# First FFN of a hybrid decoder step: weight sums on VectorE instead of GpSimd, and down pieces handed out three behind four products

## Chip, cores and metric

The kernel runs on one core of one Trainium2 chip. The metric is the device time of one execution in microseconds (us). A core has TensorE (PE in the rows, with PEld for its weight loads), VectorE (DVE), ScalarE (ACT), GpSimd (POOL) and SyncE (SP, whose queue issues the weight loads). Each engine works through its own instructions in the order in which they stand.

## The reference, cut to what matters

One layer of a decoder is computed for 512 prompt tokens and 32 sample tokens (544 columns together) with a model width of 1024. The change lies in the first of the two feed-forward blocks:

```python
def swiglu(x, wg, wu, wd):
    return (jax.nn.silu(x @ wg) * (x @ wu)) @ wd
...
    h = h + 0.5 * rmsnorm(swiglu(rmsnorm(h, norm_g[0]), wg[0], wu[0], wd[0]), norm_g[1])
```

`wg` and `wu` are 1024 x 2816 and `wd` is 2816 x 1024, all float32. The mixer (a gated linear recurrence and a latent attention over a paged cache), its output projection and a second feed-forward block follow; the change does not touch their code.

## The kernel before

**Precision.** A float32 matrix product is made of three fast products. Each operand is split into a high part (ScalarE copies it to the type `F32R`) and a low part (VectorE subtracts the high part from the source), and high x high, high x low and low x high are added up in PSUM. The helper `split` does it, at lines 168 (ScalarE) and 169 (VectorE).

**The first FFN by block products.** Tokens lie on the free axis in two halves of 272 columns. Hidden columns are taken in pairs of tiles, 256 of them, `j` = 0 to 10. For each `j` there are two calls of `tile_pair`, one for the gate weights `w_g` (result in `G`, tile `ha` or `hb`) and one for the up weights `w_u` (result in `V`). For `j` = 0 and 1 the product is made directly (`classic`). From `j` = 2 (`WARM`) on, `seven` makes the 2 x 2 block product of (2 weight tiles x 2 halves of the contraction) with (2 halves of the contraction x 2 token halves) from seven products instead of eight. That needs sums and differences of weight blocks: `S[:,0]`, `S[:,1]`, the difference left in `w2[:, lo4]`, and the one left in `w1[:, hi4]`. These are four instructions of 128 x 512, at lines 567, 568, 569 and 573. The rows call them `S<-wraw`, `S<-S,wraw`, `wraw<-wraw` and `wraw<-wraw,S`.

There are 18 calls of `seven`. Each splits its weights (`a`: `w1` itself; `s`: the two sums; `v`: `w2`; `s4`: the last difference), runs seven products into the PSUM banks `X`, `Y` and `Z`, and moves them out: `tq<-X` on ScalarE, and five additions on VectorE by `plus` (line 585: `ha<-Y,tq`, `ha<-Z,ha` and the like). A product is 12 matmuls of 128 x 128 by 272 columns. The order in one `seven` is X, Y, X, Y, Z, Y, Z; a bank that is written a second time waits for the `plus` that reads its first value.

**Between the products.** `gated` applies the SwiGLU gate to finished `G` and `V`: three ScalarE activations at lines 318 to 320 (`sit`), VectorE multiplications at lines 615 and 616, and a split into `hh` and `hl`. `down` multiplies finished hidden tiles by `w_d`. It is a generator: each step is one piece, 12 matmuls into the tile `dn` and one addition to `ma` or `mb` (line 561; for the first group a ScalarE copy, line 559). A group has 16 pieces; there are 4 groups, started in the middle of the `w_u` call at `j` = 2, 4, 6 and 8. `fill` stands behind each of the first six products of a `seven` and takes the next step of the waiting group. So between two starts of a group there are four calls of `seven`, 28 products, 24 fills and 16 pieces. This stretch is called a period below.

**Order.** The program is written out without loops. A scheduler sets the order of the instructions on each engine from priorities and buffers; `tc.issue_after` pins a few of them. Weights come by SyncE loads of 512 KB into the tile `wraw`, which has five buffers; a load waits until a buffer is free. `S` has two buffers. After `j` = 10 a last group of down products (line 685) ends the FFN, and the mixer's projection (`w_in`) starts.

Of the kernel before, what the change touches and what calls it, by code (L numbers as in the profile page):

```python
# [14 lines left out]
ALU = mybir.AluOpType  # L15
# [11 lines left out]
HM = max(HS)  # L27
W2 = T // 2
WARM = 2
DFF = 2816  # L30
NF = DFF // P
FCH = (((0, 6), (6, 6), (12, 6), (18, 4)), ((0, 6), (6, 6), (12, 5), (17, 5)))
# [75 lines left out]
def hybrid_step_kernel(  # L108
# [5 lines left out]
    nc = tc.nc  # L114
# [12 lines left out]
    def mk(shape, dt, tag, bufs=1, pool=None):  # L127
        return (pool or cur[-1]).tile(shape, dt, name=tag, tag=tag, bufs=bufs)
# [10 lines left out]
    def ps(name, tag="ps", own=False):  # L139
        if tag == "ps" and not own:  # L140
            tag = CYC[turns[0] % 4]
            turns[0] += 1
        return pp.tile([P, 512], F32, name=name, tag=tag, bufs=NPS[tag])
# [23 lines left out]
    def split(hi, lo, src, eng=None):  # L167
        nc.scalar.copy(hi, src)
        (eng or nc.vector).tensor_tensor(lo, src, f32(hi), op=ALU.subtract)  # L169
# [82 lines left out]
    def mm3(out, pairs):  # L252
        n = 0
        last = 3 * len(pairs) - 1
        for (ah, al), (bh, bl) in pairs:
            for a, b in ((ah, bh), (ah, bl), (al, bh)):
                nc.tensor.matmul(out, a, b, start=n == 0, stop=n == last)  # L257
                n += 1
# [32 lines left out]
    def wcols(w, k0, kt, c0, n=P):  # L291
        return w[k0 * P : (k0 + kt) * P, c0 : c0 + n].rearrange("(k p) f -> p k f", p=P)
# [130 lines left out]
    def parts(pair, ks):  # L423
        return [t[:, ks] for t in pair]
# [75 lines left out]
    lo4, hi4 = slice(0, 4), slice(4, 8)  # L500
# [10 lines left out]
    with scope("ffn0") as pool:  # L511
# [5 lines left out]
        def ring():  # L517
            spin[0] += 1
            names, p_ = ((("wh", "wl"), sb), (("sh", "sl"), sp))[spin[0] % 4 > 1]
            return [mk([P, 8, P], F32R, n, 2, pool=p_) for n in names]  # L520

        def classic(w, C):
            ws = [ring() for _ in range(2)]
            for i in range(2):
                split(*ws[i], w[i])
            for x in BOTH:
                bs = ((B11, B21), (U4, B22))[x]
                for i in range(2):
                    acc = ps("acc", "acc")[:, :W2]
                    mm3(acc, [((ws[i][0][:, k], ws[i][1][:, k]), [t[:, k % 4] for t in bs[k // 4]]) for k in range(KD)])  # L530
                    mark[0] = nc.scalar.copy(C[:, 2 * i + x], acc).ins

        def product(bank, a, b, first):
            for k in range(4):
                for n, (p, q) in enumerate(((0, 0), (0, 1), (1, 0))):
                    nc.tensor.matmul(bank, a[p][:, k], b[q][:, k], start=first and k + n == 0, stop=k == 3 and n == 2, skip_group_check=True)  # L536

        downs = []

        def fill(n=1):  # L540
            for _ in range(n):
                while downs and next(downs[0], None) is None:
                    downs.pop(0)

        def down(first, q0, hs):
            nf = 2 * len(hs)
            for _ in range(3):
                yield True
            for d in range(0, KD, 2):
                raw = mk([P, 8, P], F32, "wraw", 5, pool=sb).rearrange("p (k i) c -> p k i c", i=2)  # L550
                nc.sync.dma_start(raw[:, :nf].rearrange("p k i c -> p k (i c)"), wcols(w_d[0], 2 * q0, nf, d * P, 2 * P))
                for i in range(2):
                    w = [mk([P, 4, P], F32R, "d" + n, 2) for n in "hl"]
                    split(w[0][:, :nf], w[1][:, :nf], raw[:, :nf, i])
                    for x in BOTH:
                        acc = ps("dn")[:, :W2]
                        mm3(acc, [((w[0][:, k], w[1][:, k]), [t[:, k % 2, x] for t in hs[k // 2]]) for k in range(nf)])
                        if first:
                            nc.scalar.copy(mT[x][:, d + i], acc)
                        else:  # L560
                            nc.vector.tensor_tensor(mT[x][:, d + i], mT[x][:, d + i], acc, op=ALU.add)
                        yield True

        def seven(w, C, mid=None):
            w1, w2 = w
            S = mk([P, 2, 4, P], F32, "S", 2)
            nc.gpsimd.tensor_tensor(S[:, 0], w2[:, lo4], w2[:, hi4], op=ALU.add)
            nc.gpsimd.tensor_tensor(S[:, 1], S[:, 0], w1[:, lo4], op=ALU.subtract)
            nc.gpsimd.tensor_tensor(w2[:, lo4], w1[:, lo4], w2[:, lo4], op=ALU.subtract)
            a, s, v = ring(), ring(), ring()  # L570
            for ks in (lo4, hi4):
                split(*parts(a, ks), w1[:, ks])
            nc.gpsimd.tensor_tensor(w1[:, hi4], w1[:, hi4], S[:, 1], op=ALU.subtract)
            for i, ks in enumerate((lo4, hi4)):
                split(*parts(s, ks), S[:, i])
            s4 = [mk([P, 4, P], F32R, "s4" + n, 2, pool=sp) for n in "hl"]
            with tc.issue_after(mark[0]):
                for ks in (lo4, hi4):
                    split(*parts(v, ks), w2[:, ks])
                split(*s4, w1[:, hi4])  # L580
            X, Y, Z = ps("X", "acc")[:, :W2], ps("Y", "acc")[:, :W2], ps("Z")[:, :W2]
            t = mk([P, W2], F32, "tq", 2)

            def plus(i, bank, to):
                nc.vector.tensor_tensor(C[:, i], bank, to, op=ALU.add)  # L585

            product(X, parts(a, lo4), B11, True)
            mark[0] = nc.scalar.copy(t, X).ins
            fill()
            product(Y, parts(s, hi4), T2, True)  # L590
            plus(1, Y, t)
            fill()
            product(X, parts(a, hi4), B21, False)
            nc.scalar.copy(C[:, 0], X)
            if mid:
                with tc.issue_after(mark[0]):
                    mid()
            fill()
            product(Y, parts(v, lo4), T3, False)
            plus(3, Y, t)  # L600
            fill()
            product(Z, parts(s, lo4), T1, True)
            plus(3, Z, C[:, 3])
            fill()
            product(Y, parts(v, hi4), T4, False)
            plus(2, Y, t)
            fill()
            product(Z, s4, B22, False)
            plus(1, Z, C[:, 1])
# [12 lines left out]
        def tile_pair(j, src, C, mid=None):  # L622
            if j < WARM:
                classic(pairs.pop(0) if pairs else raw_pair(src, 2 * j), C)
                if mid:
                    mid()
            else:
                seven(raw_pair(src, 2 * j), C, mid)

        for j in range(NF // 2):  # L630
            if j:
                late = G, V
            G, V = (c[:, j % 2] for c in Cq)
            if j == WARM:
                with tc.issue_after(mark[0]):
                    split(*T4, r[0])
            tile_pair(j, w_g[0], G)
            if j == WARM:
                mT = {x: actslot("m", x, n=W2) for x in BOTH}
            if j:  # L640
                H = [mk([P, 2, 2, W2], F32R, n, 3) for n in ("hh", "hl")]
                with tc.issue_after(mark[0]):
                    gated(H, *late, 0)
                hs.append(H)

            def rest():
                if j:
                    gated(H, *late, 1)
                if j in (2, 4, 6, 8):
                    fill(99)  # L650
                    downs.append(down(j == 2, j - 2, hs))

            tile_pair(j, w_u[0], V, rest)
            if j in (2, 4, 6, 8):
                hs = []
            if j == 0:
                for o, p, q in ((l[0], l[1], l[0]), (l[1], r[1], l[1]), (r[1], r[1], l[0]), (r[0], r[0], r[1])):
                    nc.vector.tensor_tensor(o, p, q, op=ALU.subtract)
                for dst, o in ((T2, r[1]), (T3, l[1]), (T1, l[0])):
                    split(*dst, o)  # L660
# [98 lines left out]
    with scope("mix") as mx_:  # L759
# [286 lines left out]
        with scope("at2"):  # L1046
# [7 lines left out]
            with scope("kv"):  # L1054
# [60 lines left out]
                for i in range(5):  # L1115
                    n = P if i < 4 else TS
# [511 lines left out]
def _arrays(inputs):  # L1628
# [10 lines left out]
        "vecs": np.ascontiguousarray(vecs),  # L1639
        "w_g": g["w_ffn_gate"].reshape(2, D, DFF),  # L1640
        "w_u": g["w_ffn_up"].reshape(2, D, DFF),
        "w_d": g["w_ffn_down"].reshape(2, DFF, D),
        "w_in": g["w_in"].reshape(D, -1),
# [22 lines left out]
```

## Time and profile before

| | |
|---|---|
| Median of 3 runs | 1302.17 us (1299.69 to 1302.77) |
| The profiled execution | 1307.5 us, of which the span is 1305.7 us |
| Busy share: PE, DVE, ACT, POOL | 97%, 75%, 57%, 14% |
| Mean granted TensorE clock | 0.993 (1.00 in every stretch of the first FFN after 20 us) |
| First product of the first `seven` | 67.53 us |
| First matmul of the last down group | 367.44 us |

Times in the trace count from the start of the span. The stretch from 67.5 to 367.4 us holds the 18 calls of `seven` and the four down groups, thus all that the change edits, but for two `seven`s' weight sums that GpSimd makes at 39 to 58 us, during `classic`. The profiled execution is 5.3 us above the median of the runs.

### The profile page before, as it was taken

What the parts mean: (1) busy time and instruction counts of PE and PEld (TensorE: products, weight loads), DVE (VectorE), ACT (ScalarE), POOL (GpSimd) and SP (SyncE); (2) the same over time, 40 slices, a digit from 0 to 9 for tenths busy, and PEclk for the clock granted to TensorE, in tenths of its full rate; (3) what the DMA queues carried; (4) which work ended last, traced back from release to release, by engine and by line L of the source; (5) the groups of instructions that cost most, each with busy time, mean ns of one, the idle gap of its engine ahead of it and who ended that gap; (6) DMA issues with size and microseconds to landing.
All of it is one profiled execution on the core that took longest, in us unless ns stands there. A gap on an engine that the chain in (4) does not pass through costs nothing.

```text
span 1305.7 us, 30361 instructions
## 1 busy us (share of the span) xinstructions
PE 1270.1 (97%) x12486; PEld 1170.7 (90%) x12486; DVE 983.5 (75%) x1897; ACT 746.1 (57%) x1578; POOL 185.0 (14%) x152
## 2 busy tenths in 40 slices
PE   7999999999999999999999999999999999999998
PEld 6989999999999988888888877777777999999997
DVE  7787777777668877776766897898987878466664
ACT  6555545454376745445658655654656777554454
POOL 0343333242100000000000422222210000000000
PEclk9999999999999999999999899999999999999998
DMA  9332323322265222323232978888776746646451
GB/s 268 109 97 81 107 89 98 94 87 79 77 188 165 76 77 74 98 76 105 83 98 82 328 231 286 273 284 260 256 250 187 224 116 181 182 143 184 142 155 53
DMA packets 280106, 197.32 MB, mean 151 GB/s; under 512 B 12830, under 2 KB 271487, under 8 KB 275615
## 3 DMA queue, kind: packets, MB, share of 16 engines
q1 hardware_dynamic: 271472, 152.11, 40.0%
q0 software_dynamic: 7168, 41.95, 8.8%
q8 instruction: 98, 1.61, 0.5%
q10 hardware_dynamic: 1326, 1.32, 0.3%
q14 instruction: 42, 0.34, 0.1%
HBM read 183.45 MB, written 11.90 MB: 150 GB/s over the span
## 4 chain that ended last, share of the span: by engine, by line
PE 82%; DVE 8%; ACT 4%; issue 3%; DMA 2%; SPq 0%; POOL 0%; DVEq 0%; ACTq 0%
PE acc L257 29%; PE acc L275 18%; PE dn L257 7%; PE Y L536 5%; PE s L1367 3%; PE X L536 3%; PE Z L536 3%; PE o L1400 3%; PE acc L685 2%; PE s L1180 1%; DVE wl L169 1%; PE pa L917 1%; PE acc L286 1%; DVE wl L249 1%; ACT wh L248 1%
## 5 line engine op out<-in xcount | busy, mean ns | idle before, releaser
L248 ACT CAST wh<-wraw 128x1024 fp32r<-128x1024 f32 (+2 forms) x194 | 185.2, 957 | 190.1 <-PE acc L257 113.2
L249 DVE TENSOR_TENSOR wl<-wraw,wh 128x1024 fp32r<-128x1024 f32 (+2 forms) x194 | 214.5, 1107 | 88.1 <-ACT wh L248 85.0
L275 PE MATMUL acc<-uha,wh 128*128 128x256 f32 (+1 forms) x528 | 159.1, 302 | 0.9 <-ACT uha L205 0.9
L275 PE MATMUL acc<-uha,wl 128*128 128x256 f32 (+1 forms) x528 | 150.4, 285 | 1.8 <-DVE wl L249 1.8
L275 PE MATMUL acc<-ula,wh 128*128 128x256 f32 (+1 forms) x528 | 151.3, 287 | 0.0
L257 PE MATMUL acc<-uhb,wh 128*128 128x288 f32 (+1 forms) x432 | 128.3, 297 | 0.1
L257 PE MATMUL acc<-ulb,wh 128*128 128x288 f32 (+1 forms) x432 | 127.7, 296 | 0.1
L257 PE MATMUL acc<-uhb,wl 128*128 128x288 f32 (+1 forms) x432 | 126.9, 295 | 0.5 <-DVE wl L249 0.3
L275 PEld LDWEIGHTS acc<-uha,wh 128*128 128x128 f32 x528 | 100.0, 190 | 15.2 <-issue 13.2
L275 PEld LDWEIGHTS acc<-uha,wl 128*128 128x128 f32 x528 | 100.0, 189 | 2.8 <-DVE wl L249 2.6
L275 PEld LDWEIGHTS acc<-ula,wh 128*128 128x128 f32 x528 | 100.4, 190 | 1.0 <-issue 1.0
L257 PEld LDWEIGHTS acc<-uhb,wl 128*128 128x128 f32 x432 | 81.2, 188 | 1.2 <-DVE wl L249 1.2
L257 PEld LDWEIGHTS acc<-uhb,wh 128*128 128x128 f32 x432 | 81.0, 187 | 0.7 <-ACT wh L248 0.3
L257 PEld LDWEIGHTS acc<-ulb,wh 128*128 128x128 f32 x432 | 81.1, 188 | 0.4 <-DVE ulb L169 0.3
L257 PE MATMUL dn<-hh,dh 128*128 128x272 f32 x256 | 73.9, 289 | 2.8 <-DVE ha L585 2.8
L257 PE MATMUL dn<-hl,dh 128*128 128x272 f32 x256 | 73.7, 288 | 0.0
L257 PE MATMUL dn<-hh,dl 128*128 128x272 f32 x256 | 73.6, 288 | 0.0
L1367 PE MATMUL s<-kh,q 64*32 64x128 f32 x2560 | 55.3, 275 | 0.6 <-issue 0.6
L1345 POOL DMA_INDIRECT rraw<-pool_r,idx x32 | 35.7, 1116 | 131.7 <-DVE kh L1355 127.3
L1391 ACT COPY pbuf<-pt 32x64 f32<-32x64 f32 x192 | 46.5, 242 | 12.8 <-DVE pt L1387 10.2
L275 PE MATMUL acc<-uhb,wh 128*128 128x272 f32 x176 | 53.2, 302 | 0.0
L257 PE MATMUL acc<-hlb,wh 128*128 128x288 f32 x176 | 52.1, 297 | 0.0
(638 smaller groups left out, 4058.6 us busy)
## 6 DMA issues: line engine op xcount, KB each, us to landing
wraw<-w_g SPq DMA_DIRECT2D x66, 512.0 KB
wraw<-w_u SPq DMA_DIRECT2D x66, 512.0 KB
wraw<-w_d SPq DMA_DIRECT2D x40, 384.0 KB
wraw<-w_in SPq DMA_DIRECT2D x24, 512.0 KB
wraw<-w_d SPq DMA_DIRECT2D x32, 320.0 KB
wraw<-w_d SPq DMA_DIRECT2D x16, 512.0 KB
wraw<-w_o SPq DMA_DIRECT2D x16, 512.0 KB
xt<-x_p SPq DMA_DIRECT2D x4, 512.0 KB
```

The source lines that it names most:

```text
L169: (eng or nc.vector).tensor_tensor(lo, src, f32(hi), op=ALU.subtract)
L248: nc.scalar.copy(wh[:, :kt], w[:, :kt])
L249: nc.vector.tensor_tensor(wl[:, :kt], w[:, :kt], f32(wh[:, :kt]), op=ALU.subtract)
L257: nc.tensor.matmul(out, a, b, start=n == 0, stop=n == last)
L275: nc.tensor.matmul(acc[:, :n], a[:, k], b[:, k], start=k + i == 0, stop=k == kt - 1 and i == 2)
L286: nc.tensor.matmul(acc, a[:, k], b[:, k], start=k + i == 0, stop=k == kt - 1 and i == 2)
L536: nc.tensor.matmul(bank, a[p][:, k], b[q][:, k], start=first and k + n == 0, stop=k == 3 and n == 2, skip_group_check=True)
L685: nc.tensor.matmul(accs[x, d], wts[d][p][:, k], hs[k // 2][q][:, k % 2, x], start=k + n == 0, stop=k == nf - 1 and n == 2)
L1345: nc.gpsimd.indirect_dma_start(rraw.rearrange("p a r -> p (a r)"), None, pool_r, off)
L1367: nc.tensor.matmul(self.s[r][c * 32 : c * 32 + 32, :P], q[rs, j], kh, start=st + jj == 0, stop=st == len(JS) - 1 and jj == 1, skip_group_c ...
L1391: (nc.scalar.copy if g else nc.vector.tensor_copy)(self.p[g * 32 : g * 32 + 32, c // 2, c % 2 * 4 : c % 2 * 4 + 4, self.i * 16 : self.i * ...
L1400: nc.tensor.matmul(o[g : g + 32, :R], self.p[:, c, a], self.craw[c][:, a], start=i + c == 0 and a < 4, stop=i + c == 2 and a >= 4, skip_gr ...
```

## The change

Two edits. First, the four weight instructions of each `seven` go from `nc.gpsimd` to `nc.vector`; their shapes, operands and place in the program text stay. Second, `fill` now gathers 0.75 of a step at each call and takes a step when a whole one is owed, so it hands out three steps behind four products. The generator `down` has one empty step ahead of its first piece instead of three, and the account `owed` is set to zero when a new group starts. A group then has 17 steps. A period's 24 fills give 18; before they gave 24 for 19 steps.

```diff
+PACE = 0.75
...
-        def fill(n=1):
-            for _ in range(n):
+        owed = [0]
+
+        def fill(n=PACE):
+            owed[0] += n
+            while downs and owed[0] >= 1:
+                owed[0] -= 1
                 while downs and next(downs[0], None) is None:
                     downs.pop(0)
...
-            for _ in range(3):
-                yield True
+            yield True
...
-            nc.gpsimd.tensor_tensor(S[:, 0], w2[:, lo4], w2[:, hi4], op=ALU.add)
-            nc.gpsimd.tensor_tensor(S[:, 1], S[:, 0], w1[:, lo4], op=ALU.subtract)
-            nc.gpsimd.tensor_tensor(w2[:, lo4], w1[:, lo4], w2[:, lo4], op=ALU.subtract)
+            nc.vector.tensor_tensor(S[:, 0], w2[:, lo4], w2[:, hi4], op=ALU.add)
+            nc.vector.tensor_tensor(S[:, 1], S[:, 0], w1[:, lo4], op=ALU.subtract)
+            nc.vector.tensor_tensor(w2[:, lo4], w1[:, lo4], w2[:, lo4], op=ALU.subtract)
...
-            nc.gpsimd.tensor_tensor(w1[:, hi4], w1[:, hi4], S[:, 1], op=ALU.subtract)
+            nc.vector.tensor_tensor(w1[:, hi4], w1[:, hi4], S[:, 1], op=ALU.subtract)
...
                     fill(99)
+                    owed[0] = 0
                     downs.append(down(j == 2, j - 2, hs))
```

The scheduler makes a new order from this on PE, DVE, ACT and SP up to the last down group; behind that, apart from a few swapped neighbours, the order is the same. Lines move down by one to five (169 is 170, 561 is 565, 567 to 569 are 571 to 573, 573 is 577, 585 is 589, 615 and 616 are 619 and 620). Three places follow.

VectorE at the start of the third down group (`j` = 6, `w_u` call). Before, from the last split of the next call's weights to the addition of the first Z:

```order
L169 TENSOR_TENSOR s4l_2719<-wraw_2695,s4h_2718 128x512
L585 TENSOR_TENSOR hb_308<-Y_2573,tq_2575 128x272
L615 TENSOR_TENSOR ha_307<-ha_307,sit_2615 128x544
L616 TENSOR_TENSOR ha_307<-ha_307,hb_308 128x544
L169 TENSOR_TENSOR wl_2706<-S_2699,wh_2705 128x512
L585 TENSOR_TENSOR hb_308<-Y_2573,tq_2575 128x272
L169 TENSOR_TENSOR hl_2532<-ha_307,hh_2531 128x544
L169 TENSOR_TENSOR wl_2706<-S_2699,wh_2705 128x512
L585 TENSOR_TENSOR hb_308<-Z_2574,hb_308 128x272
```

The same place on VectorE in the changed kernel:

```order
L170 TENSOR_TENSOR s4l_2733<-wraw_2709,s4h_2732 128x512
L589 TENSOR_TENSOR hb_308<-Y_2559,tq_2561 128x272
L619 TENSOR_TENSOR ha_307<-ha_307,sit_2615 128x544
L170 TENSOR_TENSOR dl_2771<-wraw_2649,dh_2770 128x512
L620 TENSOR_TENSOR ha_307<-ha_307,hb_308 128x544
L170 TENSOR_TENSOR wl_2720<-S_2713,wh_2719 128x512
L589 TENSOR_TENSOR hb_308<-Y_2559,tq_2561 128x272
L170 TENSOR_TENSOR hl_2518<-ha_307,hh_2517 128x544
L170 TENSOR_TENSOR wl_2720<-S_2713,wh_2719 128x512
L589 TENSOR_TENSOR hb_308<-Z_2560,hb_308 128x272
```

Between the two additions of Y stands one row more, a split for a down piece; no weight sum stands there.

VectorE one call later (`j` = 7, `w_g`), before, from the last split of the next call's weights to the second addition of Y:

```order
L169 TENSOR_TENSOR s4l_2953<-wraw_2929,s4h_2952 128x512
L561 TENSOR_TENSOR mb_922<-mb_922,dn_2743 128x272
L169 TENSOR_TENSOR dl_2831<-wraw_2828,dh_2830 128x512
L585 TENSOR_TENSOR ha_307<-Y_2727,tq_2729 128x272
L615 TENSOR_TENSOR ha_307<-ha_307,sit_2921 128x544
L616 TENSOR_TENSOR ha_307<-ha_307,hb_308 128x544
L561 TENSOR_TENSOR ma_921<-ma_921,dn_2774 128x272
L169 TENSOR_TENSOR hl_2920<-ha_307,hh_2919 128x544
L169 TENSOR_TENSOR sl_2940<-S_2933,sh_2939 128x512 x2
L561 TENSOR_TENSOR mb_922<-mb_922,dn_2801 128x272
L169 TENSOR_TENSOR dl_2889<-wraw_2828,dh_2888 128x512
L585 TENSOR_TENSOR ha_307<-Y_2727,tq_2729 128x272
```

And the same place on VectorE in the changed kernel:

```order
L577 TENSOR_TENSOR wraw_2911<-wraw_2911,S_2915 128x512
L170 TENSOR_TENSOR s4l_2935<-wraw_2911,s4h_2934 128x512
L589 TENSOR_TENSOR ha_307<-Y_2741,tq_2743 128x272
L619 TENSOR_TENSOR ha_307<-ha_307,sit_2903 128x544
L565 TENSOR_TENSOR ma_921<-ma_921,dn_2774 128x272
L620 TENSOR_TENSOR ha_307<-ha_307,hb_308 128x544
L170 TENSOR_TENSOR sl_2922<-S_2915,sh_2921 128x512
L571 TENSOR_TENSOR S_3133<-wraw_3130 128x512
L565 TENSOR_TENSOR mb_922<-mb_922,dn_2801 128x272
L170 TENSOR_TENSOR hl_2902<-ha_307,hh_2901 128x544
L170 TENSOR_TENSOR sl_2922<-S_2915,sh_2921 128x512
L589 TENSOR_TENSOR ha_307<-Y_2741,tq_2743 128x272
```

The sums of weights now stand among VectorE's other work: the fourth of one call ahead of that call's `s4l`, and the first of the call after it (`S_3133<-wraw_3130`, which needs a load to have landed) five rows behind that `s4l`, whose end frees a buffer.

SyncE's queue over one period, before:

```order
L551 DMA wraw_2200<-w_d 128x4x256
L551 DMA wraw_2326<-w_d 128x4x256
L420 DMA wraw_2359<-w_g 128x8x128
L420 DMA wraw_2360<-w_g 128x8x128
L420 DMA wraw_2541<-w_u 128x8x128
L420 DMA wraw_2542<-w_u 128x8x128
L551 DMA wraw_2662<-w_d 128x4x256
L420 DMA wraw_2695<-w_g 128x8x128
L420 DMA wraw_2696<-w_g 128x8x128
L551 DMA wraw_2828<-w_d 128x4x256
L420 DMA wraw_2929<-w_u 128x8x128
L420 DMA wraw_2930<-w_u 128x8x128
```

SyncE's queue at the same place in the changed kernel:

```order
L555 DMA wraw_2234<-w_d 128x4x256
L421 DMA wraw_2325<-w_g 128x8x128
L421 DMA wraw_2326<-w_g 128x8x128
L555 DMA wraw_2413<-w_d 128x4x256
L421 DMA wraw_2527<-w_u 128x8x128
L421 DMA wraw_2528<-w_u 128x8x128
L555 DMA wraw_2649<-w_d 128x4x256
L421 DMA wraw_2709<-w_g 128x8x128
L421 DMA wraw_2710<-w_g 128x8x128
L555 DMA wraw_2828<-w_d 128x4x256
L421 DMA wraw_2911<-w_u 128x8x128
L421 DMA wraw_2912<-w_u 128x8x128
```

Each pair of gate or up loads is now followed by one down load; before, two down loads stood together once in a period and two pairs had none between them.

## The prediction

> **What bounds the kernel now.** I read the page first. TensorE is busy nearly throughout, so the change can only win back time in which TensorE waits.
>
> ```profile
> span 1305.7 us, 30361 instructions
> PE 1270.1 (97%) x12486; PEld 1170.7 (90%) x12486; DVE 983.5 (75%) x1897; ACT 746.1 (57%) x1578; POOL 185.0 (14%) x152
> ```
>
> Next the chain, for the ends of the stretch that the change edits and the length of one product.
>
> ```profile
> 67.53 1.51 PE X L536 x12
> ...
> 365.94 1.49 PE Z L536 x12
> 367.44 4.64 PE acc L685 x37
> ```
>
> A block of 12 matmuls takes 1.50 us (365.94 to 367.44) when TensorE runs through. The stretch holds 18 x 7 products and 4 x 16 pieces, 190 blocks, at least 285.0 us; it takes 299.9. So 14.9 us is all that the change could win. A view by stages tells where they lie; its columns are the stretch, its length, and busy us (x instructions) of PE, PEld, DVE, ACT and POOL, then the granted clock, DMA share and GB/s. I cut at the same Z product of each period.
>
> ```profile
> 67.50:92.80 25.30, 22.16 (x170) 21.12 (x168) 23.84 (x31) 18.05 (x34) 11.71 (x8) 1.00 0.36 105
> 92.80:161.80 69.00, 67.44 (x530) 66.60 (x531) 50.41 (x72) 37.59 (x76) 24.94 (x17) 1.00 0.31 92
> 161.80:230.90 69.10, 67.04 (x530) 66.26 (x529) 53.48 (x85) 32.53 (x60) 24.25 (x16) 1.00 0.31 92
> 230.90:300.00 69.10, 67.06 (x531) 66.28 (x530) 53.13 (x85) 32.54 (x60) 23.71 (x16) 1.00 0.31 92
> 300.00:367.40 67.40, 66.53 (x531) 66.19 (x529) 46.93 (x79) 32.37 (x59) 13.39 (x9) 1.00 0.24 70
> sum 299.90, PE 290.24 PEld 286.45 DVE 227.80 ACT 153.08 POOL 98.00; mean PE 58.05 PEld 57.29 DVE 45.56 ACT 30.62 POOL 19.60
> ```
>
> The start holds 14 blocks (21.0 us) and loses 4.3; there VectorE is busy for 23.84 of 25.30 us. Each of the three full periods holds 44 blocks (66.0 us) and loses 3.0 to 3.1; the end holds 44 and loses 1.4. The clock is 1.00 throughout. What TensorE waits for, from the groups by line (idle time and its cause stand last):
>
> ```profile
> L257 PE MATMUL dn<-hh,dh 128*128 128x272 f32 x256 | 73.9, 289 | 2.8 <-DVE ha L585 2.8
> L536 PE MATMUL Y<-t4h,sh 128*128 128x272 f32 x40 | 12.0, 300 | 3.7 <-DVE hb L585 3.1 <-DVE ha L585 0.6
> L536 PE MATMUL Y<-t3h,sh 128*128 128x272 f32 x40 | 11.9, 298 | 3.0 <-DVE hb L585 3.0
> ```
>
> Every cause is a `plus` of VectorE that comes late. One such wait in order of time, GpSimd first, then VectorE, then TensorE:
>
> ```profile
> 221.33 1.30 POOL L567 TENSOR_TENSOR S<-wraw 128x512 f32<-128x512 f32 x1 [0.78 <-DMA wraw<-w_u]
> 222.70 1.61 POOL L568 TENSOR_TENSOR S<-S,wraw 128x512 f32<-128x512 f32 x1
> 224.28 1.77 POOL L569 TENSOR_TENSOR wraw<-wraw 128x512 f32<-128x512 f32 x1
> ```
> ```profile
> 221.72 1.46 DVE L169 TENSOR_TENSOR s4l<-wraw,s4h 128x512 fp32r<-128x512 f32 x1 [2.26 <-ACT s4h L168]
> 223.10 0.43 DVE L585 TENSOR_TENSOR hb<-Y,tq 128x272 f32<-128x272 f32 x1
> 223.45 1.45 DVE L615 TENSOR_TENSOR ha<-ha,sit 128x544 f32<-128x544 f32 x1
> 224.93 1.70 DVE L616 TENSOR_TENSOR ha<-ha,hb 128x544 f32<-128x544 f32 x1
> 226.55 0.68 DVE L169 TENSOR_TENSOR wl<-S,wh 128x512 fp32r<-128x512 f32 x1
> 227.15 0.43 DVE L585 TENSOR_TENSOR hb<-Y,tq 128x272 f32<-128x272 f32 x1
> 227.50 0.71 DVE L169 TENSOR_TENSOR hl<-ha,hh 128x544 fp32r<-128x544 f32 x1
> ```
> ```profile
> 227.63 0.39 PE L536 MATMUL Y<-t4h,sh 128*128 128x272 f32 x1 [0.78 <-DVE hb L585]
> ```
>
> While GpSimd runs its three sums, three VectorE instructions take 1.45 to 1.70 us instead of some 0.7; the first one clear of GpSimd takes 0.68. The `plus` at 227.15 is late by about that, and TensorE stands.
>
> **The change part by part: removed.** The stretch of VectorE by GpSimd goes. Its size, from VectorE's groups in the stretch:
>
> ```profile
> L169 DVE TENSOR_TENSOR dl<-wraw,dh 128x512 fp32r<-128x512 f32 x30 | 29.6, 987 | 1.8 <-ACT dh L168 1.0
> L169 DVE TENSOR_TENSOR wl<-wraw,wh 128x512 fp32r<-128x512 f32 x34 | 29.2, 889 | 3.9 <-ACT wh L168 3.2
> L615 DVE TENSOR_TENSOR ha<-ha,sit 128x544 f32<-128x544 f32 x20 | 19.3, 964 | 3.2 <-ACT sit L320 3.2
> L169 DVE TENSOR_TENSOR sl<-S,sh 128x512 fp32r<-128x512 f32 x16 | 17.3, 1098 | 1.7 <-ACT sh L168 1.2
> L616 DVE TENSOR_TENSOR ha<-ha,hb 128x544 f32<-128x544 f32 x18 | 16.6, 925 | 0.4
> L169 DVE TENSOR_TENSOR wl<-S,wh 128x512 fp32r<-128x512 f32 x18 | 15.2, 849 | 2.3 <-ACT wh L168 2.0
> L169 DVE TENSOR_TENSOR s4l<-wraw,s4h 128x512 fp32r<-128x512 f32 x18 | 15.2, 844 | 32.5 <-ACT s4h L168 32.4
> L169 DVE TENSOR_TENSOR hl<-ha,hh 128x544 fp32r<-128x544 f32 x18 | 14.8, 822 | 3.2 <-ACT hh L168 3.2
> ```
> ```profile
> L169 DVE TENSOR_TENSOR sl<-S,sh x16: 687/693/1793, 103.6 to 331.8; 128x512 fp32r<-128x512 f32 x16
> ```
>
> The last line gives least, median and most for one form, in ns: 0.69 us is the undisturbed price of 128x512, and 0.71 (227.50) that of 128x544. The 116 instructions of 512 take 106.5 us, 26.5 above 116 x 0.69; the 56 of 544 take 50.7, 10.9 above 56 x 0.71. Removed: 37.4 us.
>
> The Trainium skill ("SBUF — State Buffer", section "Who interferes with whom") says that a VectorE instruction with two SBUF inputs and a GpSimd instruction that reads SBUF contend, and that the second to issue blocks fully until the first ends. The contention agrees with the rows; its size does not: GpSimd was busy for 98.0 us, and VectorE was stretched by 37.4. Taken literally the rule would free 98.0, the start would win about 2 us more, and the sum below would be 11.3 instead of 9.3; I go by the rows.
>
> **Added.** GpSimd's instructions in the stretch are these:
>
> ```profile
> L569 POOL TENSOR_TENSOR wraw<-wraw 128x512 f32<-128x512 f32 x16 | 28.0, 1747 | 0.0
> L568 POOL TENSOR_TENSOR S<-S,wraw 128x512 f32<-128x512 f32 x16 | 26.1, 1628 | 1.3
> L567 POOL TENSOR_TENSOR S<-wraw 128x512 f32<-128x512 f32 x16 | 22.7, 1418 | 86.7 <-DMA wraw<-w_g 59.0 <-DMA wraw<-w_u 27.7
> L573 POOL TENSOR_TENSOR wraw<-wraw,S 128x512 f32<-128x512 f32 x17 | 21.9, 1291 | 98.0 <-issue 36.8 <-DVE wl L169 31.6 <-DVE sl L169 29.6
> ```
>
> On VectorE, 65 x 0.69 = 44.9 us (same size, two float32 inputs in SBUF, as the splits). VectorE's work becomes 227.8 - 37.4 + 44.9 = 235.3 us, 83% of 285.0: room, but only if its waits, now 72.1 us, shrink to 49.7. The largest single one, 32.5 us before `s4l`, is such slack: a wait of 1.8 us per call for a ScalarE cast that itself waits for an X product. The seven sums that GpSimd makes at 39 to 58 us add 7 x 0.69 = 4.8 us ahead of the stretch; they lie 10 us and more before the first X product at 67.53, so I cost them at nothing, bounds 0 and 4.8.
>
> **A new wait at the head of a queue.** GpSimd waited 86.7 us for loads, which hurt nobody. On VectorE everything behind would wait. SyncE's row for one pair of loads:
>
> ```profile
> 214.86 3.09 SPq L420 DMA_DIRECT2D wraw<-w_u  x2
> ```
>
> The second load issues by 217.95 and its sum starts at 221.33: 3.4 us. In the order shown, five rows stand between the split that frees the buffer and the sum that reads it: 0.43 + 0.71 + 0.43 + 0.71 + 0.69 = 3.0 us, less overlaps of some 0.1 each, 2.6. So VectorE waits there 0.8 us by my estimate, between 0 and 3.4. The 1.8 us of slack per call covers 0.8; I cost it at nothing.
>
> **Moved.** With pieces at an even pace the piece-free products vanish (before, the last 5 of 24 fills and the first 3 empty steps gave none), so a late `plus` has more products ahead of it to hide in. In the place quoted, with quiet durations between starts, VectorE goes 0.61, 0.35, 0.75, 0.60 (the added split), 0.64, 0.60 from 221.72: the `plus` starts at 225.3 instead of 227.15, and the 0.78 us wait is gone. The first piece of a group now needs the gate's split `hl` earlier, behind the Z product; I count some 0.3 us to spare there, so a wait of up to 0.5 us may be late next, four times. The down loads, one behind each pair, carry the same bytes. GpSimd's queue loses only these 72 instructions; its gathers come later and are untouched.
>
> **Sum.** One more row, of ScalarE, bears on the start:
>
> ```profile
> L168 ACT CAST s4h<-wraw 128x512 fp32r<-128x512 f32 x18 | 11.1, 615 | 5.9 <-POOL wraw L573 5.9
> ```
>
> Start: VectorE limits it; the stretch by its 8 GpSimd instructions, at the mean of 37.4 / 65 = 0.58, is 4.6 us, about what 8 sums add (5.5), but ScalarE's `s4h` no longer waits for GpSimd (5.9 us in all): I take 1.5 of 4.3 us, between 0 and 4.3. Three periods: 2.4 of 3.1 each, leaving 0.7 for the wait just named: 7.2. End: 0.6 of 1.4. Behind the stretch nothing changes in kind. Together 9.3: the profiled execution goes from 1307.5 to 1298.2. That execution stands 5.3 above the median, so the median goes from 1302.2 to 1292.9.
>
> **The rivals.** (1) Slower: VectorE becomes the bound. If its waits stay 72.1 us because each hangs on ScalarE or a load, the stretch takes 235.3 + 72.1 = 307.4, 7.5 us more: 1309.7. It decides when the waits shrink by less than 7.5 us. For it speaks VectorE's 23.84 of 25.30 at the start; against, the `s4l` slack. The Trainium skill ("Perfetto Trace Analysis", section "Optimizing Scalar/DVE Operations") names moving work off a saturated VectorE, even to GpSimd, the reverse of this change, but adds that the shared port may spoil it. The 37.4 us bear out the second half here. Chance 0.08.
> (2) No gain: loads at the head of VectorE's queue wait 1.8 us and more, eating all slack, and late `plus` rows only move: 1301, within 0.3%. Chance 0.18.
> (3) Half: the piece-free wait goes (0.78 and the refill, some 1.2 us a period), the others stay: 4 x 1.2 = 4.8, 1297.4. Chance 0.19.
> Forecast: 0.55.
>
> **How the numbers follow.** The measurement can tell about 0.3%, 3.9 us, from no change. Faster: 0.55 and most of (3), 0.72; same 0.20; slower 0.08. The range goes from 1288 (13.9 won, nearly the whole loss) to 1301.5, which leaves out rival (1) and the tail of (2).
>
> **What would show it.** Right: GpSimd idle until the mixer; `dl`, `wl`, `sl` and lines 619 and 620 near 0.69 to 0.72 us; VectorE some 235 us busy; the periods 66.5 to 67; the last down group starting some 9 us earlier. Wrong: line 571 with long waits for loads, TensorE waiting for line 589 as before, or periods of 69. A clock below 1.00 in the stretch would spoil the comparison.

## The result, and the profile after

The changed kernel takes 1287.82 us (median of six runs, 1284.79 to 1290.58); the kernel before, timed beside it, 1302.04 us (1299.69 to 1305.43). The ratio is 0.989, with a 95% interval of 0.9871 to 0.9909. That is 14.2 us less, between 11.8 and 16.8. The forecast was 1292.9 and its range began at 1288: the direction was right and the gain was larger than I had allowed for, by 0.18 us at the range's end and by 5.1 us at the point.

The page of the changed kernel, its busy times and GpSimd's line of the 40 slices:

```profile
span 1283.0 us, 30297 instructions
PE 1256.4 (98%) x12486; PEld 1166.0 (91%) x12486; DVE 981.9 (77%) x1969; ACT 746.6 (58%) x1578; POOL 76.1 (6%) x80
...
POOL 0000000000000000000000422222310000000000
```

GpSimd does almost nothing until the mixer (1.6 us ahead of the first X product, none in the stretch), as the edit has it. VectorE has 72 instructions more (1969 against 1897), and its busy time fell by 1.6 us. The chain of waits, with the end of the stretch:

```profile
353.67 1.49 PE Z L537 x12
355.16 13.25 PE acc L690 x106
```

For all kernels below I count the stretch from the first matmul of the first X product (67.37 us before, 67.30 after) to the start of the last down group as the chain has it (367.44 and 355.16): 300.07 us before, 287.86 after. So 12.2 us were won there. A second execution of the changed kernel, further down, gave 287.60, so a difference of some 0.3 us between two stretches says nothing. The stages, cut at the same products as before; the columns are those of the prediction's table:

```profile
67.46:88.78 21.32, 21.32 (x171) 21.15 (x170) 19.78 (x35) 17.27 (x33) 0.00 (x0) 1.00 0.35 100
88.78:154.90 66.12, 66.12 (x528) 65.89 (x527) 50.56 (x89) 37.52 (x75) 0.00 (x0) 1.00 0.34 102
154.90:221.10 66.20, 66.20 (x528) 65.97 (x527) 53.75 (x101) 32.73 (x60) 0.00 (x0) 1.00 0.33 98
221.10:287.30 66.20, 66.00 (x526) 65.68 (x525) 52.87 (x99) 32.74 (x60) 0.00 (x0) 1.00 0.32 96
287.30:355.16 67.86, 67.86 (x541) 67.54 (x540) 49.77 (x94) 33.42 (x60) 0.00 (x0) 1.00 0.25 73
sum 287.70, PE 287.50 PEld 286.24 DVE 226.73 ACT 153.69 POOL 0.00; mean PE 57.50 PEld 57.25 DVE 45.35 ACT 30.74 POOL 0.00
```

TensorE is busy in 287.50 of 287.70 us. The cuts don't hold quite the same numbers of matmuls in both kernels (541 against 531 in the last stage), so I price each matmul at 1.50 / 12 = 0.125 us (a block is 12 matmuls) and call the rest of a stage its loss. Before, the losses were 4.05, 2.75, 2.85, 2.7 and 1.0 us; now they are 0, 0.1, 0.2, 0.45 and 0.2. The gain is 4.1 us at the start, 7.5 in the three periods and 0.8 at the end, 12.4 together.

VectorE's groups in the stretch:

```profile
L170 DVE TENSOR_TENSOR sl<-wraw,sh 128x512 fp32r<-128x512 f32 x36 | 23.6, 688 | 0.5
L170 DVE TENSOR_TENSOR wl<-wraw,wh 128x512 fp32r<-128x512 f32 x34 | 22.2, 688 | 3.4 <-ACT wh L169 3.3
L170 DVE TENSOR_TENSOR dl<-wraw,dh 128x512 fp32r<-128x512 f32 x30 | 20.7, 689 | 3.9 <-ACT dh L169 3.4
...
L620 DVE TENSOR_TENSOR ha<-ha,hb 128x544 f32<-128x544 f32 x22 | 15.8, 720 | 0.1
...
L170 DVE TENSOR_TENSOR s4l<-wraw,s4h 128x512 fp32r<-128x512 f32 x18 | 12.4, 692 | 16.8 <-ACT s4h L169 16.6
...
L571 DVE TENSOR_TENSOR S<-wraw 128x512 f32<-128x512 f32 x16 | 11.0, 690 | 4.3 <-DMA wraw<-w_g 3.3 <-DMA wraw<-w_u 1.0
```

`dl` went from 987 to 689 ns, `wl` from 889 to 688, and the sums cost 690 each. The first sum of a call (L571) does stand waiting for loads, but only 4.3 us in 16 calls. TensorE's groups with a wait of over 0.1 us in the stretch are one line; the prediction's three of before had 9.5 us:

```profile
L258 PE MATMUL dn<-hh,dh 128*128 128x272 f32 x256 | 74.3, 290 | 0.2 <-DVE ha L589 0.2
```

And the place of the prediction, where a `plus` came late behind lengthened instructions, on VectorE in order of time:

```profile
213.94 0.69 DVE L170 TENSOR_TENSOR s4l<-wraw,s4h 128x512 fp32r<-128x512 f32 x1
214.55 0.43 DVE L589 TENSOR_TENSOR hb<-Y,tq 128x272 f32<-128x272 f32 x1
214.90 0.71 DVE L619 TENSOR_TENSOR ha<-ha,sit 128x544 f32<-128x544 f32 x1
215.53 0.68 DVE L170 TENSOR_TENSOR dl<-wraw,dh 128x512 fp32r<-128x512 f32 x1
216.13 0.72 DVE L620 TENSOR_TENSOR ha<-ha,hb 128x544 f32<-128x544 f32 x1
216.77 0.68 DVE L170 TENSOR_TENSOR wl<-S,wh 128x512 fp32r<-128x512 f32 x1
217.37 0.43 DVE L589 TENSOR_TENSOR hb<-Y,tq 128x272 f32<-128x272 f32 x1
```

From `s4l` to the second `plus` it is now 3.43 us (213.94 to 217.37), with one split more in between; before it was 5.43 (221.72 to 227.15). Note the start times: `dl` lasts 0.68 us, but the next instruction starts 0.60 behind it.

### The profile page after: what moved, and what is told of

It is laid out like the page before. It is cut to its first block, busy times and chain, and to the rows that moved or that the text cites. A ratio compares the mean times of both kernels' runs of the same rounds, so it can differ in the third digit from the quotient of the medians.

```text
span 1283.0 us, 30297 instructions
## 1 busy us (share of the span) xinstructions
PE 1256.4 (98%) x12486; PEld 1166.0 (91%) x12486; DVE 981.9 (77%) x1969; ACT 746.6 (58%) x1578; POOL 76.1 (6%) x80
## 4 chain that ended last, share of the span: by engine, by line
PE 85%; DVE 7%; ACT 4%; DMA 2%; issue 1%; DVEq 0%; ACTq 0%
PE acc L258 30%; PE acc L276 17%; PE dn L258 7%; PE Y L537 6%; PE X L537 4%; PE Z L537 4%; PE s L1372 3%; PE o L1405 2%; PE acc L690 2%; DVE wl L250 1%; PE s L1185 1%; PE pa L922 1%; PE acc L287 1%; DVE kh L1360 1%; ACT wh L249 1%
## 5 line engine op out<-in xcount | busy, mean ns | idle before, releaser
L1396 ACT COPY pbuf<-pt 32x64 f32<-32x64 f32 x192 | 46.5, 242 | 13.3 <-DVE pt L1392 10.6
L258 PE MATMUL acc<-hhb,wh 128*128 128x288 f32 x176 | 51.8, 298 | 0.0
```

Source lines behind the costliest of these rows:

```text
L1396: (nc.scalar.copy if g else nc.vector.tensor_copy)(self.p[g * 32 : g * 32 + 32, c // 2, c % 2 * 4 : c % 2 * 4 + 4, self.i * 16 : self.i * ...
```

## The experiments

Two edits were made at once, so the first question is which of them pays: theory A says the sums, because VectorE is no longer lengthened by GpSimd; theory B says the pace.

**The sums alone.** The old `fill` and its three empty steps stay; the four sums are on VectorE.

```diff
-        owed = [0]
-
-        def fill(n=PACE):
-            owed[0] += n
-            while downs and owed[0] >= 1:
-                owed[0] -= 1
+        def fill(n=1):
+            for _ in range(n):
...
-            yield True
+            for _ in range(3):
+                yield True
```

> The four weight sums of each call are on VectorE, as in the changed kernel, but the old fill (one step behind each product, three empty steps ahead of a group) is kept. The stretch from the first X product to the last down group took 299.9 us before and 287.7 after, and 190 blocks of 1.50 us need 285.0. Theory A (the loss before was VectorE's instructions stretched by GpSimd): most of the gain is here already; stretch 288 to 290 us, start of 14 blocks 21.3 to 21.8, total 10 to 12 us below before. Theory B (the loss was the piece-free products, in which VectorE and ScalarE fall behind): the stretch stays at 295 to 299 us and the periods at 68 to 69.

Measured 1286.51 us (ratio to before 0.9885, 0.9867 to 0.9904), the stretch 287.43 us. This is the changed kernel's result without the pace, as theory A has it. VectorE's splits `wl`, `sl` and `dl` of loaded weights are at 685 to 687 ns.

**The pace alone.** The new `fill`; all four sums stay on GpSimd.

```diff
-            nc.vector.tensor_tensor(S[:, 0], w2[:, lo4], w2[:, hi4], op=ALU.add)
+            nc.gpsimd.tensor_tensor(S[:, 0], w2[:, lo4], w2[:, hi4], op=ALU.add)
...
-            nc.vector.tensor_tensor(w1[:, hi4], w1[:, hi4], S[:, 1], op=ALU.subtract)
+            nc.gpsimd.tensor_tensor(w1[:, hi4], w1[:, hi4], S[:, 1], op=ALU.subtract)
```

> The new pace of down pieces (three behind four products, one empty step), with all four weight sums on GpSimd as before. Theory A: VectorE is still stretched (128x512 splits of 0.85 to 1.1 us on the mean), the start still loses some 4 us, the stretch takes 295 to 299 us. Theory B: the periods fall to 66.5 and the stretch to some 290 us, with only the start as slow as before.

Measured 1292.35 us (0.9938, 0.9917 to 0.996), the stretch 292.92: 7.2 us of the 12.2, between what the two theories expected. Its groups show that VectorE is lengthened as much as ever:

```profile
L170 DVE TENSOR_TENSOR dl<-wraw,dh 128x512 fp32r<-128x512 f32 x30 | 33.7, 1123 | 5.3 <-ACT dh L169 4.5
...
L170 DVE TENSOR_TENSOR sl<-S,sh 128x512 fp32r<-128x512 f32 x17 | 22.9, 1371 | 1.6 <-ACT sh L169 1.5
```

And its stages (same columns) show where that still costs something:

```profile
67.20:92.00 24.80, 21.74 (x165) 20.70 (x164) 23.23 (x29) 17.16 (x32) 10.54 (x8) 1.00 0.37 107
92.00:158.00 66.00, 66.00 (x524) 65.53 (x523) 46.74 (x71) 37.48 (x75) 21.05 (x14) 1.00 0.30 91
...
224.00:290.00 66.00, 66.00 (x525) 65.62 (x524) 52.45 (x84) 32.05 (x59) 23.86 (x17) 1.00 0.31 93
```

In the periods TensorE never stops, though `dl` takes 1.12 us: the late `plus` no longer reaches it. That the pieces behind three of four products hide it fits this, but was not tested by itself. At the start, where hardly any pieces are yet to be had, TensorE still stands for 3 us. So the two edits are two cures for the periods' loss, and each is enough there; the start's loss is cured by the sums alone.

**Which sum.** VectorE could lose time at the start by being lengthened ("contention"), or because GpSimd hands the fourth sum over late ("handover"). With the even pace, first the other three sums went to GpSimd (here one of the three lines), then the fourth alone:

```diff
-            nc.vector.tensor_tensor(S[:, 0], w2[:, lo4], w2[:, hi4], op=ALU.add)
+            nc.gpsimd.tensor_tensor(S[:, 0], w2[:, lo4], w2[:, hi4], op=ALU.add)
```
```diff
-            nc.vector.tensor_tensor(w1[:, hi4], w1[:, hi4], S[:, 1], op=ALU.subtract)
+            nc.gpsimd.tensor_tensor(w1[:, hi4], w1[:, hi4], S[:, 1], op=ALU.subtract)
```

> The first three sums of a call on GpSimd as before the change, only the fourth (L577) on VectorE; the even pace stays. Theory 'handover': what the start of the stretch loses comes from VectorE waiting for GpSimd's late fourth sum, through ScalarE's s4h; then the start (first X product to the end of 14 blocks) takes about 21.5 to 22.5 us rather than the 25 of the even pace with all sums on GpSimd, and the whole stretch 289 to 290.5 us. Theory 'contention': it comes from VectorE's instructions being lengthened while GpSimd reads; three quarters of GpSimd's work is left, so the start stays at 24 to 25 us and the stretch at 292 to 293.

> The counterpart: the first three sums on VectorE, only the fourth (L577) on GpSimd, at the even pace. Theory 'handover': the last sum of the chain is still late, so the start loses 2 to 4 us and the stretch takes 290 to 292 us. Theory 'contention': a quarter of GpSimd's reading is left, so the start takes 21.5 to 22.5 us and the stretch 288 to 289 us.

Measured: 1293.56 us and a stretch of 292.30 with the fourth on VectorE, 1287.78 and 288.86 with the fourth alone on GpSimd. Both stretches are where contention puts them. The start is less clear: its 14 blocks are done 23.0 us after the first matmul with the fourth on VectorE, between the two theories, against 25.1 with all four on GpSimd; with the fourth alone on GpSimd they are done after 21.8, as contention has it. So a late fourth sum is not the main cause, though it may have a part at the start: over the whole stretch three of GpSimd's four cost nearly as much as all. In the first 21.4 us of the stretch TensorE is busy for 21.40 us with no sum on GpSimd, 20.80 with the fourth, 19.68 with the first three and 19.20 with all.

**Where.** With the even pace, the sums of the first four calls on one engine and those of the other 14 on the other. The counterpart has `> 4`, and all four sums are changed as the one shown:

```diff
...
+            calls[0] += 1
+            eng = nc.vector if calls[0] <= 4 else nc.gpsimd
...
-            nc.vector.tensor_tensor(S[:, 0], w2[:, lo4], w2[:, hi4], op=ALU.add)
+            eng.tensor_tensor(S[:, 0], w2[:, lo4], w2[:, hi4], op=ALU.add)
```

> The even pace, and the sums of the first four of the 18 calls on VectorE, those of the other 14 on GpSimd. Theory 'only the start': with an even pace the lengthening of VectorE's instructions costs TensorE time only at the start, where VectorE is busy without a break; then the first 21.4 us hold 21.2 to 21.4 us of TensorE work and the stretch takes 287.5 to 289 us, as with all sums on VectorE. Theory 'everywhere': the lengthening costs a little in each period; the stretch takes 290 to 292 us.

> The counterpart: the even pace, the sums of the first four calls on GpSimd, those of the other 14 on VectorE. Theory 'only the start': the first 21.4 us hold about 19.2 us of TensorE work and the stretch takes 291.5 to 293 us, as with all sums on GpSimd. Theory 'everywhere': it takes 288.5 to 290.5 us.

Measured: 1287.05 us and 288.55 in the stretch when only the later calls use GpSimd; 1290.51 and 291.74 when only the first four do. The first 21.4 us of each, in that order:

```profile
67.28:88.68 21.40, 21.40 (x171) 21.23 (x170) 19.69 (x35) 17.29 (x33) 0.00 (x0) 1.00 0.35 100
```
```profile
67.11:88.51 21.40, 19.24 (x148) 18.41 (x147) 19.81 (x26) 15.28 (x29) 7.21 (x5) 1.00 0.34 99
```

VectorE is busy for 19.7 to 19.8 us in both, but finishes 35 instructions in the one and 26 in the other, and TensorE gets 171 matmuls or 148. In the first kernel GpSimd then works 82.3 us, with `dl` at 1052 ns, and the stretch is 0.7 us longer than with no sum on GpSimd. That is "only the start": 3.9 us from the first four calls, 0.7 from all the others.

**Contention without a handover.** Four kernels gave GpSimd work whose result nobody needs, on top of the changed kernel. First, reading (18 copies of 128x128 per call into a spare tile), and writing (one copy and 40 memsets):

```diff
...
+            for k in range(18):
+                nc.gpsimd.tensor_copy(dum, w2[:, k % 4])
```
```diff
...
+            nc.gpsimd.tensor_copy(dum, w2[:, 0])
+            for _ in range(40):
+                nc.gpsimd.memset(dum, 0)
```

> The changed kernel, and on GpSimd in each call 18 copies of 128x128 from the loaded weights into a spare tile that nobody reads; the order on VectorE is the same as in the changed kernel. Only the contention comes back, not the handover of sums between engines. Theory A: VectorE's splits and gates are stretched again (0.69 to 0.9 us and more on the mean) and the stretch grows from 287.7 to 291 to 297 us. Theory B: 288 us, since nothing waits for GpSimd.

> The changed kernel, and on GpSimd in each call one copy of 128x128 and 40 memsets of 128x128 bytes into a spare tile that nobody reads; VectorE's order is the same as in the changed kernel. If GpSimd's reads of SBUF are what stretches VectorE, memsets, which only write, leave it alone: splits at 0.69 us, stretch 288 us. If any work of GpSimd does it, the result is as with the copies, in proportion to GpSimd's busy time.

Measured: 1286.73 us and a stretch of 289.35 reading, 1288.45 and 288.09 writing (one run each). Reading cost 1.5 us in the stretch, less than theory A asked for, and nothing in its first 21.4 us. GpSimd was busy about equally long in both, but only reading lengthened VectorE, and by little. First the group of reads and `wl` beside it, then the same of the memsets:

```profile
L576 POOL CAST dum<-wraw 128x128 uint8<-128x128 f32 x296 | 133.7, 452 | 136.1 <-DVE wraw L573 110.1 <-issue 8.1
...
L170 DVE TENSOR_TENSOR wl<-wraw,wh 128x512 fp32r<-128x512 f32 x34 | 24.4, 750 | 3.0 <-ACT wh L169 3.0
```
```profile
L577 POOL MEMSET dum<- 128x128 uint8 x679 | 138.7, 204 | 39.2
...
L170 DVE TENSOR_TENSOR wl<-wraw,wh 128x512 fp32r<-128x512 f32 x34 | 22.1, 684 | 3.5 <-ACT wh L169 3.3
```

These copies, small and with one input, lengthen VectorE less than the real sums. So, two inputs, in small pieces:

```diff
...
+            for k in range(24):
+                h = slice(k % 2 * 64, k % 2 * 64 + 64)
+                nc.gpsimd.tensor_tensor(dum, w2[:, k // 2 % 4, h], w1[:, k // 2 % 4, h], op=ALU.add)
```

> The changed kernel, in which GpSimd also makes 24 needless additions per call, each of two float32 pieces (128x64) of the weight tiles into a spare tile that nobody reads; VectorE makes all four real sums, so nothing waits for GpSimd's results. Theory 'contention': reading two inputs on GpSimd lengthens VectorE's two-input instructions as the real sums did; GpSimd is busy for some 80 to 120 us in the stretch, VectorE's 128x512 instructions average over 0.80 us, the first 21.4 us hold fewer than 20.8 us of TensorE work, and the stretch grows from 287.9 to 291 us or more. Theory 'lateness': what counts is that GpSimd delivers its sums late, and the lengthening alone is absorbed; then the stretch stays below 289.5 us and the start keeps its 21.4 us of TensorE work.

Measured 1366.95 us, and a stretch of 367.55: far outside what either theory meant, from a cause that I had not thought of. An addition of 128x64 took 496 ns, 24 of them 12 us per call, and these read the weight buffers. The waits of VectorE, and one of those of SyncE's queue:

```profile
DVE S L571 <- DMA wraw<-w_g: 50.5, 7, 13.8
...
DVE S L571 <- DMA wraw<-w_u: 30.0, 7, 6.6
```
```profile
SPq L421 <- POOL dum L577: 74.2, 15, 8.5
```

The loads waited for GpSimd to release the buffers, and VectorE stood at the first sum for the loads: 80.5 us, where the changed kernel has 4.3. That the stretch grew by nearly as much, 79.7 us, is in part chance: TensorE stood still for 59 us of it, and its own busy time rose by 20.6 us (308.1 against 287.5), at a granted clock of 0.91 behind the start. The start, ahead of these waits, kept 21.27 us of TensorE work, with GpSimd busy for 10.1 of 21.4 us; these small pieces did not slow it as the real sums did. Otherwise the run says nothing on contention, but it shows that the new wait at the head of VectorE's queue, of which the prediction spoke, can grow large when loads come late.

The last attempt holds no weight buffer, and has the real sums' shape. It works in the dead `S` tile:

```diff
             for i, ks in enumerate((lo4, hi4)):
                 split(*parts(s, ks), S[:, i])
+            for _ in range(4):
+                nc.gpsimd.tensor_tensor(S[:, 0], S[:, 0], S[:, 1], op=ALU.subtract)
```

> The changed kernel, in which GpSimd, behind the last split of S, also makes four needless subtractions per call of the real sums' shape (128x512 float32, two inputs), in the S tile, which nobody reads again before the call after next overwrites it; no weight buffer is held by them and all four real sums stay on VectorE. Theory 'contention': some 65 such instructions of 1.3 to 1.8 us in the stretch lengthen VectorE's 128x512 instructions to over 0.80 us on average; with VectorE's 65 real sums beside them the stretch grows from 287.9 to 291 us or more, with less than 20.8 us of TensorE work in the first 21.4. Theory 'lateness': only results that come late from GpSimd cost time; the stretch stays below 289.5 and the start keeps its 21.4.

Measured 1333.83 us and a stretch of 333.66, 45.8 more than the changed kernel's. The size is far beyond what I expected. The first 21.4 us of this kernel's stretch, with the columns of the stages:

```profile
68.58:89.98 21.40, 19.58 (x152) 18.97 (x151) 19.93 (x29) 16.04 (x30) 6.62 (x4) 1.00 0.35 99
```

TensorE is busy for 19.58 us there instead of 21.40, at a granted clock of 1.00, and no row of the waits names GpSimd as what an engine waited for. Contention alone is enough to cost time, without any late result. One burst of four, GpSimd first, then VectorE beside it:

```profile
166.65 6.82 POOL L581 TENSOR_TENSOR S<-S 128x512 f32<-128x512 f32 x4 [14.80 <-DVE wl L170]
```
```profile
166.49 0.68 DVE L170 TENSOR_TENSOR dl<-wraw,dh 128x512 fp32r<-128x512 f32 x1
167.10 1.82 DVE L170 TENSOR_TENSOR hl<-ha,hh 128x544 fp32r<-128x544 f32 x1
168.83 0.43 DVE L591 TENSOR_TENSOR hb<-Y,tq 128x272 f32<-128x272 f32 x1
169.19 1.43 DVE L170 TENSOR_TENSOR wl<-S,wh 128x512 fp32r<-128x512 f32 x1
170.54 0.43 DVE L591 TENSOR_TENSOR hb<-Z,hb 128x272 f32<-128x272 f32 x1
170.90 1.43 DVE L170 TENSOR_TENSOR wl<-wraw,wh 128x512 fp32r<-128x512 f32 x1
```

Nobody waits for these four, and each VectorE instruction with two inputs in SBUF that starts behind the first of them takes 1.4 to 1.8 us instead of 0.7; those with an input in PSUM keep their 0.43. VectorE now has the sums and the lengthening, 280.2 us busy against 226.7, which I take to be why the total is so large. TensorE stands still for 33.1 us of the stretch; 13.0 of the 45.8 are its own busy time, which rose as its granted clock fell to 0.95 to 0.98 behind the start.

**How much room VectorE has.** The first sum issued five times:

```diff
-            nc.vector.tensor_tensor(S[:, 0], w2[:, lo4], w2[:, hi4], op=ALU.add)
+            for _ in range(5):
+                nc.vector.tensor_tensor(S[:, 0], w2[:, lo4], w2[:, hi4], op=ALU.add)
```

> The changed kernel with the first sum of each call (L571) issued five times on VectorE instead of once: the same values, four needless 128x512 instructions more per call, some 64 to 68 in the stretch. Theory 'occupancy 0.60': one such instruction behind another costs VectorE 0.60 us, so its busy time in the stretch goes from 226.7 to about 265 to 268 of 288 us, below the bound, and the stretch grows by 0 to 3 us. Theory 'price 0.69': each costs 0.69, VectorE reaches 271 to 274 us with its order of work too rigid to use the rest, and the stretch grows by 6 us or more, to 294 or above.

```profile
sum 289.73, PE 288.09 PEld 286.38 DVE 262.43 ACT 154.80 POOL 0.00; mean PE 288.09 PEld 286.38 DVE 262.43 ACT 154.80 POOL 0.00
```

Measured 1290.61 us, the stretch 289.73: 64 instructions more cost VectorE 35.7 us (0.56 each) and TensorE 1.9. The price of a sum in a busy queue is thus not its 0.69.

**Beyond the stretch.** The changed kernel once more:

> The changed kernel itself once more, timed beside the kernel before. If the change acts in the first FFN's stretch alone, the stretch takes 287.5 to 288 us and the time is 12 us below that of the kernel before, with 1000 to 1003 us outside the stretch, as in the kernel before. If the change also shortens what follows, the time is 14 us or more below.

Measured 1288.94 us against 1302.21 (0.9901, 0.9868 to 0.9934), 13.3 less, with a stretch of 287.60, 12.5 less. In all four timed comparisons the time fell by 0.8 to 2.0 us more than the stretch (14.2 and 12.2; 13.3 and 12.5; the sums alone 13.9 and 12.6; the pace alone 8.0 and 7.2). Each of these differences is inside its interval, and the stretch of before is known from one execution only. The six runs of the changed kernel differ by 5.8 us among themselves, and what lies outside the stretch takes 995.1 to 999.5 us in the profiles of the changed kernel and its variants, 1005.6 in the one profile of before. Whether a little is won elsewhere stays open.

The kernels compared, in one table (us; the time is the median, or the one run where there was one; the rest is from one profile each, "busy" within the stretch, "PE, start" in its first 21.4 us):

| sums on VectorE | pace | time | stretch | PE, start | VectorE busy | GpSimd busy |
|---|---|---|---|---|---|---|
| none (before) | old | 1302.04 | 300.07 | 19.00 | 227.8 | 98.0 |
| none | even | 1292.35 | 292.92 | 19.20 | 226.4 | 97.3 |
| the fourth | even | 1293.56 | 292.30 | 19.68 | 227.7 | 72.7 |
| all, from call 5 | even | 1290.51 | 291.74 | 19.24 | 228.9 | 13.5 |
| the first three | even | 1287.78 | 288.86 | 20.80 | 220.9 | 22.8 |
| all, to call 4 | even | 1287.05 | 288.55 | 21.40 | 220.0 | 82.3 |
| all (the change) | even | 1287.82 | 287.86 | 21.40 | 226.7 | 0 |
| all | old | 1286.51 | 287.43 | 21.40 | 226.8 | 0 |

No version beats the changed kernel by more than the measurement tells.

## Why the prediction was off, point by point

**The place and the mechanism were right.** Late `plus` rows behind lengthened VectorE instructions cost the time; the lengthening is gone (all groups of 512 and 544 elements with two SBUF inputs at 686 to 722 ns), GpSimd idles until the mixer, TensorE's waits at L589 are down to 0.2 us, and the last down group starts 12.3 us earlier, where I had said some 9.

**The term that was mis-sized is the start: 1.5 us forecast, 4.1 won.** It holds 2.6 of the 2.9 us by which the stretch did better than 9.3. The step read: 8 GpSimd instructions at the mean of 0.58 us lengthen VectorE by 4.6, about what 8 sums add, 5.5. Both numbers were wrong for that place. The same 25.3 us, before and after:

```profile
67.37:92.67 25.30, 22.29 (x170) 21.24 (x168) 23.71 (x31) 18.00 (x33) 11.58 (x8) 1.00 0.36 105
```
```profile
67.30:92.60 25.30, 25.30 (x202) 25.13 (x201) 23.60 (x42) 19.33 (x36) 0.00 (x0) 1.00 0.34 98
```

In the same busy time VectorE now finishes 42 instructions instead of 31, more than the 8 sums that it took over. Counted row by row, the 22 instructions of 512 and 544 elements in that window were 7.2 us longer than undisturbed ones (16 by 4.3 us, 6 by 2.9), 0.90 per GpSimd instruction. As I read it, the mean over the whole stretch counts many GpSimd instructions that ran while VectorE waited, and at the start it hardly waits. And 8 sums add 8 x 0.60 = 4.8 us. That makes a gain of 2.4 us where I had seen a loss of 0.9. The remaining 1.7 of the 4.1 I can't attribute term by term. That the lengthening alone, beside VectorE's own sums, costs TensorE 1.8 us in 21.4 is shown by the dead subtractions; how much the sums' own lateness adds was not separated.

**The range's end.** I had set it at 1288 as 13.9 us won, but 1288 lies 14.2 below 1302.2. The 12.2 us won in the stretch would by themselves have stayed inside the range; the time passed its end only with the 2.0 us outside the stretch, which no run explains. That it passed the end at all is thus chance. That the forecast missed by 5.1 us is the start's 2.6, these 2.0 and small rests.

**Added: 44.9 us was the wrong kind of price.** I took 0.69 us, the duration of one instruction; in a queue the next one starts 0.60 us later, as the rows at 215.53 and 216.13 show. I had used such start-to-start times for the quoted place, where the forecast of 3.6 us from `s4l` to the `plus` met 3.43, but not in the sum. VectorE is 226.7 us busy, not 235.3, and its waits had to shrink only from 72.1 to 61.0 us. At 0.60 the 65 sums add 39.0 us and the same sum gives 229.4; the other 2.7 us I can't account for. The Trainium skill ("VectorE: DVE Perf Modes", section "The TRN2 errata — SBUF-src ops pay a fixed extra latency per instruction") gives (N+151)/0.96 ns for a float32 addition, 691 for 512 elements, and 58 + N cycles in its table, an estimate of 594 ns; here the first is the duration and the second the distance between starts.

**The periods: 7.2 forecast, 7.5 won.** The size was right. That a first `hl` would be late next by up to 0.5 us, four times, was not: TensorE waits 0.2 us in all. The reason I gave, sums and pace together, was more than was needed: either edit alone takes the wait away.

**The end: 0.6 forecast, 0.8 won.**

**Costed at nothing.** The first sum's wait for loads: 4.3 us in 16 calls, 0.27 each, where I had estimated 0.8; it stays hidden, so nothing was the right cost. The kernel whose loads come late shows that the place is a real one. The sums ahead of the stretch: the first X product starts at 67.30 us, before at 67.37. But in the second execution of the changed kernel it starts at 69.87, so a cost of up to some 2.5 us there is not excluded.

**The rivals.** VectorE did not become the bound. With 53.4 us more work in bursts (the dead subtractions) TensorE stands still for 33.1 us, with 35.7 (the repeated sum) for 1.6. No gain and half the gain are out by the interval. Outside the stretch I forecast nothing, and nothing is shown.

**The literal rule came nearer.** By the Trainium skill ("SBUF — State Buffer", section "Who interferes with whom") a VectorE instruction with two SBUF inputs and a GpSimd instruction that reads contend, and neither one that only writes nor a VectorE instruction with at most one SBUF input does. The runs agree on all three counts: reads lengthen, memsets do not, an instruction with a PSUM input keeps its 0.43 us. Its word (the same page of the Trainium skill, section "SBUF: two separate sides") that the other "fully blocks" I had priced at 11.3 us and set aside for 9.3; the stretch won 12.2. I had set it aside because 37.4 us of lengthening is less than GpSimd's 98.0 us of work. The burst above, where both engines have work, looks close to taking turns (four lengthened VectorE instructions beside four of GpSimd), though a VectorE instruction is lengthened by 0.74 to 1.1 us, and not by a GpSimd instruction's whole 1.7.

## What to carry to other kernels

A mean taken over a whole stretch prices contention wrongly where it matters: count the lengthening in the stage in which the slowed engine has no pauses; here it was 0.90 us per GpSimd instruction there and 0.58 on the mean. Price an instruction that is added to a busy queue by the distance between starts, not by its duration. And when two edits cure the same wait, try each alone before adding up their gains; here the pace is worth 7.2 us without the sums and nothing with them.

## What the runs showed of the hardware

GpSimd's 128x512 subtractions, which read two inputs, lengthen a VectorE instruction with two SBUF inputs from some 0.7 to 1.4 to 1.8 us when both run back to back, and leave one with a PSUM input at 0.43; 139 us of GpSimd memsets lengthen nothing (684 ns for `wl`). A 128x128 copy on GpSimd took 355 ns where there was one per call and 452 ns where 18 stood in a row; why was not tested. An addition of 128x64 on GpSimd took 496 ns and one of 128x512 some 1.3 to 1.7 us: eight times the elements for about three times the time.
